# Two large constants moved to the front of the constant pool, and one narrow constant widened to 96 bytes

## The chip, the cores and the metric

The kernel runs on one core of a Trainium2 chip. The time is device microseconds (us) of one execution. Before the change the median of three runs is 2517.71 us (2516.28 to 2519.01). Engines are called as the profile calls them: PE is the matmul engine (PEld is its weight load), DVE the vector engine, ACT the scalar engine, POOL GpSimd, SP the engine that issues the DMAs.

## The reference

A decoder trunk of two layers on one sequence of 1024 tokens, model width 1024, all in float32. Every layer is: RMS norm, token mixer, residual add, RMS norm, gated MLP with a causal convolution of width 3, residual add. A final RMS norm follows.

```python
for layer in range(2):
    hn = rms_norm(h, norm_mix[layer])
    if layer == 0:
        h = h + diff_attention(hn, ...)   # 8 heads, two score maps per head, rotary positions
    else:
        h = h + gla(hn, ...)              # gated linear attention, 4 heads
    h = h + conv_ffn(rms_norm(h, norm_ffn[layer]), ...)   # 1024 -> 2 x 2816 -> 1024
return rms_norm(h, norm_final)
```

Most of the arithmetic is in the dense products: the projections of the mixers and the two matrices of each MLP.

## The kernel before

**Three matmuls for one.** Every float32 product is made of two parts with fewer bits, high and low. `mm3` (L141 to L144) adds three matmuls into one place of PSUM:

```python
nc.tensor.matmul(ps, lhsT=ah, rhs=bh, start=first, stop=False)   # L142
nc.tensor.matmul(ps, lhsT=ah, rhs=bl, start=False, stop=False)   # L143
nc.tensor.matmul(ps, lhsT=al, rhs=bh, start=False, stop=last)    # L144
```

The first operand (`lhsT`) is stationary: 128 columns of it are loaded into the array ahead of each matmul, which the profile shows as an LDWEIGHTS on PEld. The second (`rhs`) is the moving operand and streams through, mostly 512 numbers in each of 128 partitions, that is 2048 bytes of each partition. In the profile a matmul is named output<-moving,stationary: `psq<-XH,wh` streams XH against the weight `wh`.

**Where things lie in SBUF.** Each partition is laid out by tile pools one behind the other, in the order in which they are opened (L52 to L55): `const`, `wpool`, `small`, `slots`. Within a pool the tiles follow each other in the order in which the program asks for them first, and each takes a multiple of 32 bytes. As built, the first constant begins at byte 16,512 of every partition, and then

| what | bytes of a partition | begins at | over a multiple of 64 by | over a multiple of 512 by |
|---|---|---|---|---|
| `ident`, `ones_f`, `ones` | 512 each | 16,512 | 0 | 128 |
| `mhalf` (a column of -0.5) | 4, takes 32 | 18,048 | 0 | 128 |
| `XH` | 32,768 | 18,080 | 32 | 160 |
| `XL` | 32,768 | 50,848 | 32 | 160 |
| `sub`, `ls`, `lam`, `cv`, `gn`, `ba` | 864 in all | 83,616 | 32 | 160 |
| `wpool`: `st` x3, `wh` x2, `wl` x2 | 4,096 each | 84,480 | 0 | 0 |
| `small` (columns of statistics) | 1,088 | 113,152 | 0 | 0 |
| `slots`: 28 common places | 4,096 each | 114,240 | 0 | 64 |

All rows within XH, XL, `wpool` and the places begin at a whole multiple of 512 bytes from the start of their tile, so that the last column holds for every operand that is cut from them.

**XH and XL** are the normalized activations, transposed (feature in the partition, token in the row), as high and low part: 8 blocks of 1024 tokens. `norm_to_X` (L197) and `Blocks` (L234, L244) fill them. They are then the moving operand of

- the projections of both mixers, `project_T` (L146): q and k of the attention and of the GLA (`psq`), the attention's values (`psv`, 512 wide) and the GLA's gate (`psr`), each against weights in `wpool`. In `project_tok` (L153, the GLA's values, `psv` 256 wide) they are stationary instead;
- the up-projection of the MLP, `ffn` (L521). It is computed by Strassen's scheme in the variant of Winograd: seven products per pair of feature tiles instead of eight. `product` (L526) takes one of seven blocks of the activations and one of seven blocks of the weights. Four activation blocks (A11, A12, A22, S1) are cut from XH and XL, three (S2, S3, S4; `S` in the profile) lie in common places. Of every 11 weight blocks 7 lie in common places (`uw`) and 4 in `wpool` (`wh`, `wl`), by turns (L489).

**In the down-projection** XH and XL are free and serve as two more sets of places: `places` (L614) gives, for every sixth pair of feature tiles and the next, XH and XL both as stationary (the hidden activations) and as moving operand (the weights). The other four sets are common places (`gh`, `gl`, `wdh`, `wdl`). Two or three sets take turns within one accumulation (`pacc`, L318).

```python
n = f % 6
if n < 4:
    return [slot(i, z, F32R) for i, z in zip(DOWN[layer][n], ("gh", "gl", "wdh", "wdl"))]
return [z[:, 2 * (n - 4) + i, :] for i in range(2) for z in (XH, XL)]
```

**The order of the work.** The program is written out flat. The scheduler (L1344) orders instructions by its model of their times; in the up-projections and the output projections the order on PE is pinned by `in_order` (L135). All DMAs are issued on SP. Raw weights are loaded into `st` and split by ACT (the high part) and POOL (the low part).

`mhalf` is the exponent of the inverse square root in the norms: a POOL power of 128x1 numbers (L174, L191).

Of the kernel before, what the change touches and what calls it, by code (L numbers as in the profile page):

```python
# [10 lines left out]
F32 = mybir.dt.float32  # L11
F32R = mybir.dt.float32r
# [6 lines left out]
P = 128  # L19
D = 1024  # L20
T = 1024
NT = T // P
KT = D // P
# [23 lines left out]
def trunk(ctx, tc, x, norm_mix, norm_ffn, norm_final, wqk, wv, w_o, lam_in, subln,  # L47
# [4 lines left out]
    const = ctx.enter_context(tc.tile_pool(name="const", bufs=1))  # L52
# [4 lines left out]
    psm = ctx.enter_context(tc.tile_pool(name="psm", bufs=4, space=PSUM))  # L57
    dram = ctx.enter_context(tc.tile_pool(name="dram", bufs=1, space=DRAM))

    ident = const.tile([P, P], F32, name="ident")  # L60
    ones_f = const.tile([P, P], F32, name="ones_f")
    nc.vector.memset(ones_f, 1.0)
    ones = const.tile([P, P], F32R, name="ones")
    nc.vector.tensor_copy(ones, ones_f)
    mhalf = const.tile([P, 1], F32, name="mhalf")
    nc.vector.memset(mhalf, -0.5)
    XH = const.tile([P, KT, T], F32R, name="XH")
    XL = const.tile([P, KT, T], F32R, name="XL")

    o_scr = dram.tile([2 * HEADS, P, T], F32, name="o_scr")  # L70
    h_scr = dram.tile([NT, P, D], F32, name="h_scr")
# [3 lines left out]
    def f32(ap):  # L75
        return ap.bitcast(F32)

    def slot(i, name, dt=F32, shape=None):

        return slots.tile(shape or [P, 1024], dt, name=name, tag=f"s{i}")  # L80
# [60 lines left out]
    def mm3(ps, ah, al, bh, bl, first, last, **kw):  # L141
        nc.tensor.matmul(ps, lhsT=ah, rhs=bh, start=first, stop=False, **kw)  # L142
        nc.tensor.matmul(ps, lhsT=ah, rhs=bl, start=False, stop=False, **kw)  # L143
        nc.tensor.matmul(ps, lhsT=al, rhs=bh, start=False, stop=last, **kw)  # L144

    def project_T(ps, w, hf):  # L146

        wh, wl = (z.rearrange("p (k c) -> p k c", k=KT) for z in w)
        for k in range(KT):
            mm3(ps, wh[:, k, :], wl[:, k, :], XH[:, k, half(hf)], XL[:, k, half(hf)],  # L150
                k == 0, k == KT - 1)

    def project_tok(ps, w2, t):  # L153

        for k in range(KT):
            wh, wl = (z.rearrange("p (k c) -> p k c", k=4) for z in w2[k // 4])
            tok = slice(t * P, (t + 1) * P)
            mm3(ps, XH[:, k, tok], XL[:, k, tok], wh[:, k % 4, :], wl[:, k % 4, :],
                k == 0, k == KT - 1)

    def half(hf):
        return slice(512 * hf, 512 * hf + 512)
# [34 lines left out]
    def norm_to_X(hn, t):  # L197
        for g in range(2):
# [5 lines left out]
            dst = (slice(None), slice(4 * g, 4 * g + 4), slice(t * P, (t + 1) * P))  # L204
            nc.scalar.copy(XH[dst], pv)
            nc.vector.tensor_tensor(XL[dst], pv, f32(XH[dst]), op=ALU.subtract)

# [4 lines left out]
    class Blocks:  # L212
# [5 lines left out]
        def parts(self, n):  # L218
# [3 lines left out]
            d, tok = {"A11": (0, 0), "A12": (4, 0), "A22": (4, 1), "S1": (0, 1)}[n]  # L222
            return [[(0, X[:, d:d + 4, half(tok)])] for X in (XH, XL)]

# [15 lines left out]
        def first_row(self, h0, t):  # L240
# [4 lines left out]
            pv = pt.rearrange("p (a b) -> p a b", a=KT)  # L245
            hi, lo = (z[:, :, t * P:(t + 1) * P] for z in (XH, XL))
            nc.scalar.copy(hi, pv)
# [273 lines left out]
    def ffn(layer, X, last_blocks, up, gain_src, after):  # L521
# [92 lines left out]
        def places(f):  # L614
# [6 lines that stand above are left out]
# [727 lines left out]
```

## Time and profile before

| | |
|---|---|
| median of three runs | 2517.71 us (2516.28 to 2519.01) |
| profiled execution, device time | 2519.34 us |
| its span, first to last instruction | 2517.6 us |
| mean granted PE clock | 0.991 |
| PE busy, matmuls | 2450.1 us (97%), 11752 |
| PEld busy | 1995.8 us (79%) |
| DVE, POOL, ACT busy | 1625.7, 1189.4, 1040.6 us |
| DMA queue of SP | 226.64 MB, 27.3% of 16 engines |

The stages on the time axis: norm and first projections (to about 50 us), attention (to 490), its output projection (to 620), the first MLP's up-projection (to 1050) and down-projection (to 1340), the GLA with its output projection (to 1870), the second MLP's up-projection (to 2270), its down-projection and the final norm.

A matmul's row has a start and a length. Matmuls overlap: the next one starts before the row of the last one ends, so that the pace of PE is the distance from start to start, and a stretch of PE that shows as busy can still run at a better or a worse pace.

### The profile page before, as it was taken

The numbers are of one execution on the slowest core, as the hardware profiler recorded it, in microseconds if no ns is written. First come the engines' busy times: TensorE is split into PE (matmuls) and PEld (weight loads), VectorE is DVE, ScalarE is ACT, GpSimd is POOL, SyncE is SP. The second block draws the span as 40 slices with busy tenths as digits, with TensorE's granted clock in tenths as the row PEclk, the third lists the DMA queues.
The fourth block names the chain that finished last, engine by engine and source line by source line (L and its number), as shares of the span: only waits on it lengthen the run. The fifth ranks groups of instructions, "written<-read, shape, count | busy, mean of one in ns | idle before, by whom it ended". The sixth has DMA issues, their size and how long they took to land. (4 is left out here: it accounts for less than half of the span.)

```text
span 2517.6 us, 30784 instructions
## 1 busy us (share of the span) xinstructions
PE 2450.1 (97%) x11752; PEld 1995.8 (79%) x11752; DVE 1625.7 (65%) x2210; ACT 1040.6 (41%) x1630; POOL 1189.4 (47%) x723
## 2 busy tenths in 40 slices
PE   7999999998999999999999999999899999999998
PEld 6777777776788888878888998987678888887887
DVE  5577777877666666654565486487676666655455
ACT  4454544544454554432124443442345445443211
POOL 4444444425655555554423344343465555545441
PEclk9999999999999999999999999999999999999999
DMA  5222222433222222343321111124322222244331
GB/s 188 56 67 59 59 59 59 126 122 126 75 76 84 76 85 83 137 157 109 101 87 60 34 43 59 35 92 156 112 76 76 84 77 88 79 147 148 107 101 67
DMA packets 66020, 228.60 MB, mean 91 GB/s; under 512 B 8145, under 2 KB 8785, under 8 KB 65873
## 3 DMA queue, kind: packets, MB, share of 16 engines
q1 hardware_dynamic: 65872, 226.64, 27.3%
q8 instruction: 92, 1.51, 0.3%
q14 instruction: 56, 0.45, 0.1%
HBM read 163.17 MB, written 50.86 MB: 85 GB/s over the span
## 5 line engine op out<-in xcount | busy, mean ns | idle before, releaser
L325 DVE TENSOR_TENSOR res<-pacc,res 128x512 f32<-128x512 f32 x368 | 252.9, 690 | 238.1 <-PE pacc L144 237.6
L497 POOL TENSOR_TENSOR uw<-st,uw 128x512 fp32r<-128x512 f32 x190 | 290.9, 1532 | 219.8 <-ACT uw L496 212.1
L123 POOL TENSOR_TENSOR wl<-st,wh 128x1024 fp32r<-128x1024 f32 x57 | 146.0, 2568 | 203.6 <-ACT wh L122 203.6
L144 PE MATMUL pacc<-wdh,gl 128*128 128x512 f32 x512 | 200.8, 392 | 0.0
L143 PE MATMUL pacc<-wdl,gh 128*128 128x512 f32 x512 | 200.5, 392 | 0.0
L142 PE MATMUL pacc<-wdh,gh 128*128 128x512 f32 x512 | 198.6, 392 | 1.8 <-DVE res L316 1.8
L576 DVE SCALAR_TENSOR_TENSOR b<-cu,cv,b 128x1023 f32<-128x1023 f32 x44 | 63.4, 1440 | 172.5 <-ACT b L575 172.2
L496 ACT CAST uw<-st 128x512 fp32r<-128x512 f32 x190 | 118.0, 622 | 123.8 <-PE ps_z L144 54.2
L142 PE MATMUL psq<-XH,wh 128*128 128x512 f32 x384 | 156.6, 408 | 0.1
L143 PE MATMUL psq<-XL,wh 128*128 128x512 f32 x384 | 154.1, 401 | 0.1
L144 PE MATMUL psq<-XH,wl 128*128 128x512 f32 x384 | 152.6, 399 | 0.0
L626 POOL TENSOR_TENSOR gl<-st,gh 128x1024 fp32r<-128x1024 f32 x32 | 77.8, 2430 | 151.3 <-ACT gh L625 108.4
L779 ACT ACTIVATE p<-p,nmax 128x256 f32<-128x256 f32 (+7 forms) x128 | 99.1, 777 | 85.4 <-DVE nmax L776 84.2
L497 POOL TENSOR_TENSOR wh<-st,wh 128x512 fp32r<-128x512 f32 x56 | 87.1, 1555 | 80.8 <-ACT wh L496 80.8
L625 ACT CAST gh<-st 128x1024 fp32r<-128x1024 f32 x32 | 33.6, 1050 | 202.7 <-PE pacc L143 144.1
L497 POOL TENSOR_TENSOR wl<-st,wl 128x512 fp32r<-128x512 f32 x56 | 85.3, 1524 | 63.0 <-ACT wl L496 63.0
L142 PEld LDWEIGHTS pacc<-wdh,gh 128*128 128x128 f32 x512 | 96.1, 188 | 23.4 <-DVE res L316 2.6
L143 PEld LDWEIGHTS pacc<-wdl,gh 128*128 128x128 f32 x512 | 96.1, 188 | 21.7
L144 PEld LDWEIGHTS pacc<-wdh,gl 128*128 128x128 f32 x512 | 96.1, 188 | 20.9
L776 DVE CUSTOM_DVE_ANT_0 p<-s_ps,mask 128x256 f32<-128x256 f32 (+7 forms) x128 | 91.4, 750 | 30.7 <-PE pta L802 22.4
L142 PE MATMUL pacc<-wh,gh 128*128 128x512 f32 x256 | 103.2, 409 | 4.0 <-DVE res L325 4.0
L143 PE MATMUL pacc<-wl,gh 128*128 128x512 f32 x256 | 102.8, 403 | 1.5 <-POOL wl L123 1.5
(363 smaller groups left out, 7358.9 us busy)
## 6 DMA issues: line engine op xcount, KB each, us to landing
st<-in_wup_dram SPq DMA_DIRECT2D x88, 512.0 KB, 3.5
g_scr<-a SPq DMA_DIRECT2D x44, 512.0 KB, 2.6
st<-in_wdn_dram SPq DMA_DIRECT2D x44, 512.0 KB, 3.6
st<-g_scr SPq DMA_DIRECT2D x44, 512.0 KB, 3.3
r_scr<-res SPq DMA_DIRECT2D x24, 512.0 KB, 4.7
res<-r_scr SPq DMA_DIRECT2D x24, 512.0 KB, 5.7
st<-in_wqk_dram SPq DMA_DIRECT2D x16, 512.0 KB, 3.5
st<-o_scr SPq DMA_DIRECT2D x13, 512.0 KB, 3.3
```

The lines of the kernel that those rows point to most:

```text
L123: (eng_lo or nc.gpsimd).tensor_tensor(lo, st, f32(hi), op=ALU.subtract)
L142: nc.tensor.matmul(ps, lhsT=ah, rhs=bh, start=first, stop=False, **kw)
L143: nc.tensor.matmul(ps, lhsT=ah, rhs=bl, start=False, stop=False, **kw)
L144: nc.tensor.matmul(ps, lhsT=al, rhs=bh, start=False, stop=last, **kw)
L325: nc.vector.tensor_tensor(res[t][:, half(dh)], ps, res[t][:, half(dh)], op=ALU.add)
L496: nc.scalar.copy(w[:, half(0)], src)
L497: nc.gpsimd.tensor_tensor(w[:, half(1)], src, f32(w[:, half(0)]), op=ALU.subtract)
L576: nc.vector.scalar_tensor_tensor(u[:, 1:], c[:, :T - 1], cv[:, n, 1:2], u[:, 1:], op0=ALU.mult, op1=ALU.add)
L625: nc.scalar.copy(hi, st)
L626: nc.gpsimd.tensor_tensor(lo, st, f32(hi), op=ALU.subtract)
L776: nc.vector.tensor_tensor_reduce(out=pm[:, :w], in0=s_ps[:, :w], in1=st["mask"][:, T - w:], scale=-0.125, scalar=3.0e38, op0=ALU.add, op1= ...
L779: nc.scalar.activation(pm[:, :w], pm[:, :w], AF.Exp, bias=nmax, scale=-1.0, accum_out=sums[:, m:m + 1])
```

## The change

XH and XL are asked for ahead of the narrow constants, and `mhalf` becomes the first column of a tile of 24 numbers, 96 bytes, in place of 4. No instruction is added, removed or given another shape; what changes is where tiles lie.

```diff
+    XH = const.tile([P, KT, T], F32R, name="XH")
+    XL = const.tile([P, KT, T], F32R, name="XL")
     ident = const.tile([P, P], F32, name="ident")
     ones_f = const.tile([P, P], F32, name="ones_f")
     nc.vector.memset(ones_f, 1.0)
     ones = const.tile([P, P], F32R, name="ones")
     nc.vector.tensor_copy(ones, ones_f)
-    mhalf = const.tile([P, 1], F32, name="mhalf")
+    mhalf = const.tile([P, 24], F32, name="mhalf")[:, :1]
     nc.vector.memset(mhalf, -0.5)
-    XH = const.tile([P, KT, T], F32R, name="XH")
-    XL = const.tile([P, KT, T], F32R, name="XL")
```

## The prediction

> **What bounds the kernel now.** I read the page's busy times first, then the busy time by stage, then who PE waits for.
>
> ```profile
> PE 2450.1 (97%) x11752; PEld 1995.8 (79%) x11752; DVE 1625.7 (65%) x2210; ACT 1040.6 (41%) x1630; POOL 1189.4 (47%) x723
> PEclk9999999999999999999999999999999999999999
> ```
>
> PE is busy for 97% of the span and no other engine for more than 65%; the granted clock is at 90% or more in every slice. In the stages (columns: stretch, its length, then busy time and instructions of PE, PEld, DVE, ACT, POOL):
>
> ```profile
> 50.00:490.00 440.00, 429.81 (x2156) 332.74 (x2155) 320.96 (x640) 215.56 (x442) 214.83 (x147) 0.99 0.27 74
> 620.00:1050.00 430.00, 422.81 (x1818) 341.64 (x1817) 283.81 (x275) 212.79 (x317) 240.70 (x157) 0.98 0.24 81
> 1050.00:1340.00 290.00, 288.94 (x1286) 235.70 (x1285) 160.14 (x220) 73.16 (x90) 115.43 (x54) 1.00 0.36 121
> 1340.00:1830.00 490.00, 475.11 (x2839) 413.28 (x2838) 318.61 (x425) 195.07 (x277) 214.48 (x115) 0.99 0.22 73
> 1870.00:2270.00 400.00, 399.90 (x1725) 323.94 (x1724) 259.60 (x244) 196.20 (x279) 214.62 (x137) 1.00 0.27 94
> ```
>
> In the up-projections (620 to 1050, 1870 to 2270) and the down-projection PE has nearly no gap: these stages last as long as their matmuls. In attention (50 to 490) and the GLA (1340 to 1830) it idles for 2 to 3%, and rows stretched by waits add to that. What PE waits for is little, the longest sum first:
>
> ```profile
> PE pt L202 <- DVE hn L179: 12.5, 4, 8.3
> ...
> PE s_ps L766 <- DMA ks<-kl: 2.4, 1, 2.4
> ```
>
> For a DMA it waits once, for 2.4 us. So a change that adds no instruction can move the time by one thing above all: the pace at which matmuls follow each other.
>
> **The pace is not the same everywhere.** All matmuls quoted from here on stream 512 numbers against 128 columns. From the timeline (start us, length us, the rest), the first and the last row of three runs without a gap:
>
> ```profile
> 1158.13 0.39 PE L142 MATMUL pacc<-wdh,gh 128*128 128x512 f32 x1
> ...
> 1164.93 0.39 PE L142 MATMUL pacc<-wdh,gh 128*128 128x512 f32 x1
> ```
> ```profile
> 661.12 0.40 PE L142 MATMUL ps_z<-XH,uw 128*128 128x512 f32 x1
> ...
> 663.93 0.39 PE L142 MATMUL ps_x<-S,wh 128*128 128x512 f32 x1
> ```
> ```profile
> 695.58 0.40 PE L142 MATMUL ps_x<-XH,wl 128*128 128x512 f32 x1
> ...
> 698.39 0.40 PE L142 MATMUL ps_x<-S,wl 128*128 128x512 f32 x1
> ```
>
> With both operands in common places 30 matmuls take 6.80 us, 226.7 ns each. With XH and XL moving, 12 take 2.81 us, 234.2 ns each, against weights in places (`uw`) as in `wpool` (`wl`). The groups by line and shape show that this holds throughout (after the bar: busy us, mean length of one in ns; three lines are one triple):
>
> ```profile
> L142 PE MATMUL ps_z<-S,uw 128*128 128x512 f32 x112 | 43.7, 390 | 0.0
> L144 PE MATMUL ps_z<-S,uw 128*128 128x512 f32 x112 | 43.6, 390 | 0.0
> L143 PE MATMUL ps_z<-S,uw 128*128 128x512 f32 x112 | 43.6, 389 | 0.0
> ...
> L144 PE MATMUL ps_z<-XH,uw 128*128 128x512 f32 x112 | 44.4, 396 | 0.0
> L143 PE MATMUL ps_z<-XL,uw 128*128 128x512 f32 x112 | 44.2, 395 | 0.0
> L142 PE MATMUL ps_z<-XH,uw 128*128 128x512 f32 x112 | 44.2, 394 | 0.0
> ...
> L142 PE MATMUL ps_z<-XH,wh 128*128 128x512 f32 x32 | 12.7, 397 | 0.0
> L144 PE MATMUL ps_z<-XH,wh 128*128 128x512 f32 x32 | 12.7, 396 | 0.0
> L143 PE MATMUL ps_z<-XL,wh 128*128 128x512 f32 x32 | 12.7, 396 | 0.0
> ...
> L142 PE MATMUL ps_z<-S,wl 128*128 128x512 f32 x32 | 12.7, 396 | 0.0
> L144 PE MATMUL ps_z<-S,wl 128*128 128x512 f32 x32 | 12.7, 395 | 0.0
> L142 PE MATMUL ps_z<-S,wh 128*128 128x512 f32 x32 | 12.6, 393 | 0.0
> L143 PE MATMUL ps_z<-S,wl 128*128 128x512 f32 x32 | 12.6, 393 | 0.0
> L143 PE MATMUL ps_z<-S,wh 128*128 128x512 f32 x32 | 12.5, 391 | 0.0
> L144 PE MATMUL ps_z<-S,wh 128*128 128x512 f32 x32 | 12.5, 390 | 0.0
> ```
>
> A row's length is its pace plus about 162 ns (389.7 beside 226.7, 395.0 beside about 234), so a difference of lengths is, to 2 ns, a difference of pace. Same line, output and shape: places against places 389.7; XH and XL against places 395.0; places against `wpool` 393.0; XH and XL against `wpool` 396.3. What differs is where the operands lie.
>
> **Which property of the place?** Beginnings over a multiple of 512 bytes: places 64, `wpool` 0, XH and XL 160. In the down-projection and the output projections:
>
> ```profile
> L142 PE MATMUL pacc<-wdh,gh 128*128 128x512 f32 x512 | 198.6, 392 | 1.8 <-DVE res L316 1.8
> ...
> L144 PE MATMUL pacc<-XH,XL 128*128 128x512 f32 x192 | 76.0, 397 | 0.0
> L142 PE MATMUL pacc<-XH 128*128 128x512 f32 x192 | 75.6, 394 | 0.0
> L143 PE MATMUL pacc<-XL,XH 128*128 128x512 f32 x192 | 75.1, 391 | 0.0
> ```
> ```profile
> L142 PE MATMUL pacc<-wh,gh x256: 387/394/792, 492.5 to 1818.5; 128*128 128x512 f32 x128
> ...
> L143 PE MATMUL pacc<-XL,XH x192: 387/393/397, 1096.3 to 2476.6; 128*128 128x512 f32 x192
> ```
>
> (The second fence has minimum, median and maximum.) With both operands in XH and XL a matmul comes down to 387 ns, as short as any, and yet the places that take turns with them rise to 392. `wpool` moving against places has the median 394 though it begins on a multiple of 64. So "begins on a multiple of 64" isn't what decides alone. What fits every row is that a moving and a stationary row cost little where both begin at the same place within 512 bytes, more the further they differ: difference 0 (places) 389.7, +64 (places against `wpool`) 393.0, +96 and +160 (XH against either) 395.0 and 396.3.
>
> **The change part by part.** XH moves from 18,080 to 16,512 and XL from 50,848 to 49,280; `mhalf` takes 96 bytes instead of 32, so all behind it moves up by 64: `wpool` to 84,544, the places to 114,304. Over a multiple of 512 that makes XH and XL 128, places 128, `wpool` 64. The common places were on multiples of 64 already; only XH and XL weren't. Places and `wpool` keep their distance, so their rows keep their cost. XH and XL stand to the places as the places do to each other (0) and to `wpool` as the places do (+64). Where each ends:
>
> - Up-projections, XH and XL against places: 2 layers x 22 pairs x 4 products x 12 matmuls = 2112, of which 7/11 = 1344; 395.0 to 389.7 gives 5.3 ns each, 7.1 us. All on the path.
> - The same against `wpool`, 768: 396.3 to 393.0, 3.3 ns, 2.5 us, on the path.
> - Projections of attention and GLA: `psq` 1152, `psv` 384, `psr` 384, 1920 in all, at 3.3 ns 6.3 us. The median of `psq` below agrees with 396.3. Here PE shares the end with DVE and ACT chains: I take two thirds, 4.2, between 0 and 6.3.
> - Down-projection: 576 in XH and XL at a mean of 394.0 to 389.7, 2.5 us; of 1536 beside them at 392, 2.3 ns over 389.7, 3.5 us, I take half, since some excess will have other causes: 1.8.
>
> ```profile
> L142 PE MATMUL psq<-XH,wh x384: 391/397/796, 20.1 to 1632.8; 128*128 128x512 f32 x192
> ```
>
> The other engines read and write XH and XL too, and the columns of -0.5 are read by POOL:
>
> ```profile
> L626 POOL TENSOR_TENSOR gl<-st,gh x32: 2391/2416/2657, 1046.6 to 2455.9; 128x1024 fp32r<-128x1024 f32 x32
> L626 POOL TENSOR_TENSOR XL<-st,XH x24: 2392/2408/3291, 1085.8 to 2414.1; 128x1024 fp32r<-128x1024 f32 x24
> ```
> ```profile
> L174 POOL TENSOR_TENSOR rs<-ms,mhalf x39: 544/549/1614, 5.9 to 2508.8; 128x1 f32<-128x1 f32 x39
> ```
>
> The same subtraction takes 2416 ns into a place and 2408 into XL: nothing to gain there. The power keeps its 128x1 form; I put it and the DMAs' new destinations at nothing, since PE waits for a DMA for 2.4 us in all; were all forty powers dearer by a tenth and on the path, it would be 40 x 0.055 = 2.2 us.
>
> Sum: 7.1 + 2.5 + 4.2 + 4.3 = 18.1 us. The profiled execution took 2519.34 us, so 2501.2; the median of the runs lies 1.6 below it, so 2499.6, rounded **2500 us**. Bounds: only a third of the sum, 2512; all of every term, and XH against `wpool` down to 389.7 (2688 x 6.6 = 17.7), with 7.1 and 6.0: 30.8 us, 2487.
>
> **Rivals.**
>
> *The moving row alone decides, by where it begins within 128 bytes.* Now the places begin 64 over, `wpool` 0, XH and XL 32 over; 64 would be the good one. For it: `wpool` moving has 394 where places have 389.7. Then the change turns the good value over from the places to `wpool`: 1008 matmuls of the up-projections go from 389.7 to 395.0 (5.3 us), 576 from 393.0 to 396.3 (1.9), 1536 of the down-projection from 392 to 395.0 (4.6), and some 528 with `wpool` moving gain 5 ns (2.6). Together 9.2 us: **2527 us, slower**. Against it: the 387 of XL, a moving row 32 over, and the places' 392 beside XH. It decides if the first triple above, places against places, comes out at 395.
>
> *The beginning doesn't matter; what does is the tile or its region,* which stays nearly where it was. Then 2518, no change. Against it: the places, which begin 1 KB behind `wpool`'s end, have another pace than it. The Trainium skill, SBUF — State Buffer, section Specifications (TRN2), gives lines of 16 bytes, of which every beginning here, before and after, is a multiple. TensorE: Matmul & The Clock Gate, Part 2, says that PE has two separate read ports, so that loading the next weights takes nothing from the running matmul. By either the sum would be 0 and the time stay; the 5.3 ns between rows of one shape disagree with the two taken as the whole story.
>
> *A smaller gain,* 5 to 8 us: the pace improves by the multiple of 64 alone, or phases within a triple eat the rest; 2511.
>
> **How the numbers follow.** The forecast has 0.60, the smaller gain 0.10, no change 0.15, the slower one 0.15. A measurement tells about 0.2% (5 us) from no change: faster 0.70, same 0.15, slower 0.15. The forecast's own range is 2487 to 2512; taking in the smaller gain and no change, 2490 to 2521 leaves out the slower rival and the far low end.
>
> **What would show it.** Right: XH and XL moving in `ps_z` at about 390 against `uw` and 393 against `wh`, `psq` at a median of 393 to 394, the `pacc` triples of XH at 390, places against places still 389.7, the second up-projection some 5 us shorter than 400. Wrong: `ps_z<-S,uw` at 395, or `ps_z<-XH,uw` unmoved, or a better pace of PE that comes back as waits for DVE or ACT in attention.

## The result and the profile after

The changed kernel takes 2487.57 us (median; 2486.8 to 2489.78), the kernel before, on the same chip, 2517.01 us. The ratio is 0.9889, 95% interval 0.9877 to 0.9901: 29.4 us less, where 18 were forecast: just below the low end of the range on record (2490), and at the end of the forecast's own range (2487). All matmuls stand in the same order on PE, so the two traces can be laid over each other instruction by instruction; lines of the kernel after stand one higher (L143 to L145 for the triple). Its profiled execution took 2486.8 us. Two executions are in none of the figures below, one of the changed kernel that took 2670 us at a granted clock of 0.848 and one of the kernel before that took 7827 us.

The page of the kernel after, its busy times and the granted clock:

```profile
PE 2410.0 (97%) x11752; PEld 1986.8 (80%) x11752; DVE 1631.9 (66%) x2210; ACT 1037.3 (42%) x1630; POOL 1195.9 (48%) x723
PEclk9999999999999999999999999999999999999999
```

The share of PE is the same 97%: the span shrank because PE does the same 11752 matmuls in less time, 40.1 us less, and not because it waits less. It waits more: the span less PE's busy time was 67.5 us before and is 75.0 us now, so that the span is only 32.6 us shorter. Where the gain came from, the busy times by stage show. The edges are set at the same instructions at which the stages were cut before, so that each row holds the same work (the length of the stretch is the first number behind the edges):

```profile
49.52:483.96 434.44, 422.51 (x2156) 330.61 (x2155) 319.66 (x640) 215.45 (x442) 217.53 (x147) 1.00 0.27 75
615.02:1036.09 421.07, 412.86 (x1818) 339.14 (x1817) 287.51 (x275) 211.16 (x317) 243.83 (x157) 0.99 0.24 83
1036.09:1321.89 285.80, 284.64 (x1286) 235.66 (x1285) 159.85 (x220) 73.16 (x90) 115.11 (x54) 1.00 0.37 123
1321.89:1806.89 485.00, 467.62 (x2839) 408.56 (x2838) 318.59 (x424) 194.57 (x275) 211.68 (x114) 0.99 0.22 72
1848.44:2241.12 392.68, 392.68 (x1724) 323.99 (x1724) 262.87 (x243) 194.55 (x279) 216.15 (x137) 1.00 0.28 95
...
483.96:615.02 131.06, 121.95 (x586) 96.40 (x584) 94.28 (x152) 54.14 (x95) 43.97 (x33) 0.97 0.36 119
1806.89:1848.44 41.55, 35.22 (x154) 28.47 (x153) 29.14 (x29) 18.47 (x34) 27.03 (x18) 0.93 0.21 75
2241.12:2485.00 243.88, 236.00 (x1040) 194.74 (x1038) 129.76 (x178) 53.80 (x62) 100.68 (x48) 0.99 0.31 104
```

The last of these stretches, in the kernel before:

```profile
2270.00:2517.60 247.60, 239.70 (x1040) 194.72 (x1038) 129.79 (x178) 53.79 (x62) 100.57 (x48) 1.00 0.31 102
```

Against the stretches before (440, 430, 290, 490, 400, 130, 40 and 247.6 us) attention gains 5.6 us, the up-projections 8.9 and 7.3, the down-projections 4.2 and 3.7 and the GLA 5.0; 0.5 comes from the first 50 us. The two stretches with the output projections give back 1.1 and 1.6 (the first at a granted clock of 0.97, before 0.99). Together that is 32.5 us, the difference of the two profiled executions (2519.34 and 2486.8).

Not all of it is the change. The traces record stretches in which the granted clock was half of the full one: up to the last matmul 44.4 us of them before and 30.7 us after. The matmuls that start in or beside them took 5.3 us less in the kernel after, 3.0 of it in attention and 2.5 in the first up-projection. The pad alone (below), with all distances as before, has 37.5 us of such stretches, so they vary without any change of distance. The medians, 29.4 us apart, rest on several runs.

The three runs of the forecast, at the same instructions, in the timeline of the kernel after (start us, length us):

```profile
1142.64 0.39 PE L143 MATMUL pacc<-wdh,gh 128*128 128x512 f32 x1
...
1149.44 0.39 PE L143 MATMUL pacc<-wdh,gh 128*128 128x512 f32 x1
...
653.88 0.39 PE L143 MATMUL ps_z<-XH,uw 128*128 128x512 f32 x1
...
656.60 0.39 PE L143 MATMUL ps_x<-S,wh 128*128 128x512 f32 x1
...
688.51 0.39 PE L143 MATMUL ps_x<-XH,wl 128*128 128x512 f32 x1
...
691.25 0.39 PE L143 MATMUL ps_x<-S,wl 128*128 128x512 f32 x1
```

Places against places: 30 in 6.80 us, 226.7 ns, as before. XH and XL against places: 12 in 2.72 us, 226.7 ns (234.2 before). XH and XL against `wpool`: 12 in 2.74 us, 228.3 ns (234.2 before). In the groups by line and shape:

```profile
L144 PE MATMUL pacc<-wdl,gh 128*128 128x512 f32 x512 | 198.9, 389 | 0.0
...
L143 PE MATMUL pacc<-XH 128*128 128x512 f32 x192 | 74.7, 389 | 0.0
...
L145 PE MATMUL pacc<-XH,XL 128*128 128x512 f32 x192 | 74.4, 389 | 0.0
...
L143 PE MATMUL ps_z<-S,uw 128*128 128x512 f32 x112 | 43.7, 390 | 0.0
...
L143 PE MATMUL ps_z<-XH,uw 128*128 128x512 f32 x112 | 43.6, 389 | 0.0
...
L143 PE MATMUL ps_z<-XH,wh 128*128 128x512 f32 x32 | 12.5, 392 | 0.0
...
L143 PE MATMUL ps_z<-S,wh 128*128 128x512 f32 x32 | 12.5, 392 | 0.0
```

XH and XL now have the lengths of the places beside which they stand: 389 against `uw`, 392 against `wh`, 389 in the down-projection, where also the places between them came down, from 392 to 389 or 390. Places against places stay at 389 to 390, which alone ends the rival of a moving row that decides by itself. The longest of PE's waits, and its one wait for a DMA, are about what they were (us in total, times, longest; 12.5 and 2.4 before). Waits for ACT and DVE between them grew (the two lines in the middle were 3.7 and 1.1 before):

```profile
PE pt L203 <- DVE hn L180: 12.7, 4, 8.8
...
PE ps_x L143 <- ACT rv L557: 5.2, 2, 2.7
PE ssp L295 <- DVE hl L286: 4.5, 9, 1.1
...
PE s_ps L767 <- DMA ks<-kl: 2.6, 1, 2.6
```

By stage, the stretch less PE's busy time went from 10.2 to 11.9 us in attention, from 14.9 to 17.4 in the GLA and from 4.2 to 6.3 in the short stretch ahead of the second up-projection.

### The profile page after: what moved, and what is told of

It reads as the page before. It is cut to its first block, busy times and chain, and to the rows that moved or that the text cites. A ratio compares the mean times of both kernels' runs of the same rounds, so it can differ in the third digit from the quotient of the medians.

```text
span 2485.0 us, 30784 instructions
## 1 busy us (share of the span) xinstructions
PE 2410.0 (97%) x11752; PEld 1986.8 (80%) x11752; DVE 1631.9 (66%) x2210; ACT 1037.3 (42%) x1630; POOL 1195.9 (48%) x723
## 5 line engine op out<-in xcount | busy, mean ns | idle before, releaser
L143 PE MATMUL pacc<-wdh,gh 128*128 128x512 f32 x512 | 197.9, 390 | 1.9 <-DVE res L317 1.9
L145 PE MATMUL pacc<-wdh,gl 128*128 128x512 f32 x512 | 199.3, 389 | 0.0
L497 ACT CAST uw<-st 128x512 fp32r<-128x512 f32 x190 | 117.9, 621 | 114.4 <-PE ps_z L145 50.9
L143 PE MATMUL psq<-XH,wh 128*128 128x512 f32 x384 | 154.7, 403 | 0.1
L145 PE MATMUL psq<-XH,wl 128*128 128x512 f32 x384 | 150.7, 394 | 0.0
L143 PEld LDWEIGHTS pacc<-wdh,gh 128*128 128x128 f32 x512 | 96.1, 188 | 22.5 <-DVE res L317 2.7
L145 PEld LDWEIGHTS pacc<-wdh,gl 128*128 128x128 f32 x512 | 96.1, 188 | 20.1
L143 PE MATMUL pacc<-wh,gh 128*128 128x512 f32 x256 | 103.6, 411 | 4.0 <-DVE res L326 4.0
```

What stands on the lines that cost most here:

```text
L497: nc.scalar.copy(w[:, half(0)], src)
```

## The experiments

The theories, in short. **A**, the forecast's: what counts is the distance from the beginning of the stationary row to that of the moving row, over a multiple of 512. **B**: rows are cheap where they begin on a multiple of 64 bytes. **C**: the moving row alone decides, by its place within 128 bytes.

### The law, measured by itself

This kernel leaves the trunk out. 48 matmuls of each kind run on two tiles that begin a whole multiple of 512 bytes apart; the moving rows begin `dm` numbers, the stationary rows `ds` numbers behind a multiple of 512 bytes from the start of their tile. `P` is 128, `n` 512 and `count` 48; the cut shows the loop alone.

```diff
+            for j in range(count):
+                a, b = ds + P * (j % 8), dm + 512 * (j % 8)
+                nc.tensor.matmul(ps[:, :n], lhsT=st[:, a:a + P], rhs=mv[:, b:b + n], start=j == 0, stop=j == count - 1)
```

> Leaves the whole trunk out (it copies rows of x to the output) and streams nothing but matmuls of one shape, 128 columns stationary against 512 moving numbers: 48 in a row for each pair of beginnings, the moving row shifted by 0 to 480 bytes in steps of 32 with the stationary row fixed (m.sa), the stationary row shifted with the moving one fixed (mas.), both shifted together (m.s. with equal letters), the moving row shifted by 4, 8, 16 and 24 bytes (mv_one, two, four, six), and the first series again with 256 moving numbers (half). Theory A (the difference of the two beginnings counts, zero is best): all pairs with equal letters run at 226 to 227 ns like masa, also those that begin 32 over a multiple of 64; shifts of one of the two cost 2 to 10 ns, about 2 at +64 and 6 at -64. Theory B (what counts is that the moving row begins on a multiple of 64 bytes): every second letter of the moving row is slow by 5 ns or more whatever the stationary row does, mbsb and mdsd too, and moves by 64 or 128 bytes cost nothing. Theory C (the moving row alone counts, 64 over a multiple of 128 is best): masc to maso are all alike, and the moving series alternates with a period of 128 bytes.

Its timeline has one row for each kind (start, us from the first start to the last end). The letter behind `m` is the place of the moving row, that behind `s` of the stationary one: a is 0, b 32 bytes, c 64, e 128, g 192, i 256; `mv_one` is 4 bytes:

```profile
24.05 11.04 PE L49 MATMUL masa<-mv,st 128*128 128x512 f32 x48
34.93 11.37 PE L49 MATMUL mbsa<-mv,st 128*128 128x512 f32 x48
46.13 11.16 PE L49 MATMUL mcsa<-mv,st 128*128 128x512 f32 x48
...
68.34 11.36 PE L49 MATMUL mesa<-mv,st 128*128 128x512 f32 x48
...
113.16 11.05 PE L49 MATMUL misa<-mv,st 128*128 128x512 f32 x48
...
213.47 11.36 PE L49 MATMUL masc<-mv,st 128*128 128x512 f32 x48
...
258.27 11.16 PE L49 MATMUL masg<-mv,st 128*128 128x512 f32 x48
...
369.53 11.08 PE L49 MATMUL mbsb<-mv,st 128*128 128x512 f32 x48
...
533.24 11.42 PE L49 MATMUL mv_one<-mv,st 128*128 128x512 f32 x48
```

Less the last row's length (0.39 us) and divided by 47, the pace is 226.6 ns at distance 0, 233.6 at 32 bytes, 229.1 at 64, 233.4 at 128, 226.8 at 256. With the stationary row at 64 (distance -64) it is 233.4, at 192 (-192, which is +64 over a multiple of 256) 229.1. Both rows 32 bytes off a multiple of 64: 227.4. Four bytes of distance already cost the full price, 234.7. So B and C fall here: in a stream of one kind only the distance counts, and it counts over a multiple of **256**, not 512. "More the further they differ" falls too: there are three prices, about 227 at 0, 229 at +64, and 232 to 235 at everything else tried. Each kind ran once, in one execution.

### Half of the change: the order alone, the pad alone

The order of the changed kernel, with `mhalf` narrow again (XH and XL 128, places 64, `wpool` 0 over a multiple of 512):

```diff
-    mhalf = const.tile([P, 24], F32, name="mhalf")[:, :1]
+    mhalf = const.tile([P, 1], F32, name="mhalf")
```

> XH and XL first, mhalf left at 4 bytes: XH and XL begin 128 over a multiple of 512, the places 64, the weight pool 0, all on multiples of 64; XH stands 64 above the places and 128 above the weight pool. Theory A: XH against places goes from 226.9 back to about 229 to 230 ns a matmul and to 233 where XH is stationary, XH against the weight pool (128 apart) is unknown between 229 and 234; the time 2495 to 2512. Theory B: all begins are on multiples of 64, so the time is that of the changed kernel, 2488 within 4. Theory C: places stay at the good 64, only XH is as slow as before: about 2517.

Measured: 2509.34 us (2506.33 to 2511.25), ratio 0.9967 (0.9954 to 0.9979). Every row lies on a multiple of 64 as in the changed kernel, and about three quarters of the gain are missing; B wanted 2488. XH and XL now stand 64 from the places and 128 from `wpool`.

The pad alone, in the order of before (XH and XL 224, places 128, `wpool` 64: all distances as before):

```diff
-    mhalf = const.tile([P, 1], F32, name="mhalf")
+    mhalf = const.tile([P, 24], F32, name="mhalf")[:, :1]
```

> mhalf widened, the order of before: XH and XL begin at 224 over a multiple of 512, the places at 128, the weight pool at 64; every difference is that of the kernel before, and XH is still 32 over a multiple of 64. Theory A and theory B: 2517 within 4, no change from before. Theory C: the places lose the good 64, slower, about 2527.

Measured: 2518.1 us (2515.26 to 2518.92), ratio 1.0 (0.9991 to 1.0009). Everything behind `mhalf` moved by 64 bytes and nothing changed. C, which wanted 2527, falls in the trunk as well. The pad does nothing by itself; with the new order it brings XH and XL to distance 0 from the places.

### All in one phase

The pad at 40 numbers, and one tile of statistics with two buffers instead of four, which shortens `small` by 64 bytes: XH, XL, places and `wpool` all at 128.

```diff
-    mhalf = const.tile([P, 24], F32, name="mhalf")[:, :1]
+    mhalf = const.tile([P, 40], F32, name="mhalf")[:, :1]
...
-        ss = small.tile([P, 2], F32, name="ss2")
+        ss = small.tile([P, 2], F32, name="ss2", bufs=2)
```

> Order of the change, mhalf at 160 bytes and the column pair ss2 with two buffers instead of four, so that XH, XL, the weight pool and the places all begin 128 over a multiple of 512. Theory A: matmuls with one operand in the weight pool fall to 227 as well: 2688 from 229.4 (6.5 us), 576 from 228.9 (1.1), 528 from 233.4 (3.4), 11 us in all, 2477. Theory B and theory C: 2488 within 4, as the changed kernel.

Measured: 2484.5 us (2481.56 to 2488.3), ratio 0.9866 (0.985 to 0.9882). A's forecast of 2477 was too low, B's 2488 too high by as little as the measurement tells, so this run separates nothing. The next does: the same, but with everything 32 bytes past a multiple of 64 (`mhalf` ahead of XH, 40 numbers behind `ones_f`).

```diff
+    mhalf = const.tile([P, 1], F32, name="mhalf")
     XH = const.tile([P, KT, T], F32R, name="XH")
     XL = const.tile([P, KT, T], F32R, name="XL")
...
-    ones_f = const.tile([P, P], F32, name="ones_f")
+    ones_f = const.tile([P, P + 40], F32, name="ones_f")[:, :P]
...
-    mhalf = const.tile([P, 24], F32, name="mhalf")[:, :1]
...
-        ss = small.tile([P, 2], F32, name="ss2")
+        ss = small.tile([P, 2], F32, name="ss2", bufs=2)
```

> XH/XL, common places and wpool slots all begin 32 bytes past a multiple of 64, and all at the same phase (160 past a multiple of 512): no row lies on a multiple of 64, but every distance is 0. Theory A (distance modulo 256 decides): as the one-phase kernel on multiples of 64, 2482 to 2488 us. Theory B (multiples of 64 decide, as the change says of itself): no gain, 2515 to 2520 us.

Measured: 2484.6 us (2484.09 to 2485.42), ratio 0.9873 (0.9858 to 0.9888). Not one of these rows begins on a multiple of 64, and the kernel is as fast as the one on multiples of 64. B is refuted; a beginning on a multiple of 64 is not the cause of the gain. Groups by line and shape of this kernel:

```profile
L143 PE MATMUL ps_z<-XH,uw 128*128 128x512 f32 x112 | 43.6, 389 | 0.0
...
L143 PE MATMUL ps_z<-XH,wh 128*128 128x512 f32 x32 | 12.4, 389 | 0.0
```

Even `wh`, at 392 in the changed kernel, comes down to 389, since its distance is 0 now. The changed kernel itself, beside it on the same chip:

> The changed kernel once more, beside the variants of this job, to compare them on one chip: 2487 us by every theory.

Measured: 2487.38 to 2489.65 us, ratio 0.9887 (0.9872 to 0.9902). All four runs of the one-phase kernel 32 bytes off lie below these, by some 4 us, though the intervals of the two ratios overlap. A's count for one phase was 11 us. In the trace of the kernel 32 bytes off PE's idle time is 78.5 us, against 75.0 in the changed kernel; whether the faster matmuls or the two buffers for `ss2` caused that, no run separates.

### XH and XL moved away again, by 128 and by 256 bytes

Places and `wpool` at distance 0 of each other, XH and XL 128 away from both, all on multiples of 64 (`mhalf` 72 numbers wide), and then 256 away (104 wide). Against the changed kernel:

```diff
-    mhalf = const.tile([P, 24], F32, name="mhalf")[:, :1]
+    mhalf = const.tile([P, 72], F32, name="mhalf")[:, :1]
...
-        ss = small.tile([P, 2], F32, name="ss2")
+        ss = small.tile([P, 2], F32, name="ss2", bufs=2)
```

> XH/XL at 128, places and wpool slots at 256 past a multiple of 512: all on multiples of 64, places and slots at distance 0 of each other, XH/XL at distance 128 from both. Theory A: the pairs of XH/XL with slots and places cost 233.4 ns instead of 226.7 to 228.9, 1376 with places by 6.5 and 2688 with slots by 4.2 ns = 20 us more than the changed kernel, the place-slot pairs (576 + 1536 by 2 to 4.5 ns = 8 us at most) are cheaper: 2497 to 2510 us. Theory B: all on multiples of 64, as the changed kernel, 2487 us or a little less.

Measured: 2504.85 us (2503.85 to 2506.38), ratio 0.9953 (0.994 to 0.9965), within A's 2497 to 2510 and far from B's 2487. By group:

```profile
L143 PE MATMUL ps_z<-XH,uw 128*128 128x512 f32 x112 | 44.2, 395 | 0.0
...
L143 PE MATMUL ps_z<-XH,wh 128*128 128x512 f32 x32 | 12.6, 395 | 0.0
...
L143 PE MATMUL ps_z<-S,wh 128*128 128x512 f32 x32 | 12.4, 389 | 0.0
```

> XH/XL at 128, places and slots at 384 past a multiple of 512: XH/XL 256 bytes away from both. If the distance counts modulo 512, as the prediction took it, XH/XL pairs pay the full 233.4 ns and the kernel takes 2500 to 2510 us, as with a distance of 128. If it counts modulo 256, as the single pairs showed, this is the one-phase kernel: 2482 to 2488 us.

Measured: 2484.53 us (2478.79 to 2485.8), ratio 0.9867 (0.9847 to 0.9887). A period of 512 bytes wanted 2500 to 2510. So in the trunk, too, the distance counts over a multiple of 256. Between these two kernels only the distance of XH and XL to all the rest differs, by 128 bytes: 20 us.

### Whose stationary row, and how wide

PEld is busy for 80% of the changed kernel's span and PE for 97%, so stationary rows are loaded while matmuls run. Does the distance to a matmul's own stationary row count, or that to the next one's? Here two kinds of stationary rows alternate, 128 bytes apart (64 in `own_quarter`, which is built like `own`); the trunk is left out. `dm` and `ds` are pairs now, in numbers of 4 bytes; the cut shows three of the kinds and the line that picks the rows.

```diff
+    yield "own", (0, 32), (0, 32), 512, COUNT
+    yield "next", (32, 0), (0, 32), 512, COUNT
...
+    yield "half", (0, 0), (0, 32), 512, COUNT
...
+                a, b = ds[j % 2] + P * (j % 8), dm[j % 2] + 512 * (j % 8)
```

> The trunk is left out again: 48 matmuls of each kind on two tiles of random rows, outputs not the trunk's. Two kinds of stationary rows alternate, at 0 and at 128 bytes. Theory A with the distance to the matmul's OWN stationary rows: 'own' (moving rows follow their own: 0, 128) runs at 226.7 ns, 'next' (moving 128, 0: distance 128 to its own, 0 to the rows loaded for the next matmul) at 233.4 ns, 'half' (moving always 0) at the mean, 230. Rival, the distance to the stationary rows that are LOADED DURING the matmul, which are the next one's: 'next' 226.7, 'own' 233.4, 'half' 230. The quarter kinds (distance 64 bytes between the two stationaries): own 226.7 against next 228.9 to 233.4, or the other way round. By size (128, 256, 384, 512 columns), distance 0, 64 and 128: a cost by column would give 3.3 ns at 256 columns where 512 have 6.7; a cost by load of 128 columns would give the same ns at each size, unless the load hides. After 48 matmuls at a distance of 160 bytes, 48 at distance 0 in eight groups of 6: if the rows get well at once, all groups run at 226.7 ns; if a lag lingers, as the unchanged place-by-place rows of the trunk suggest (228.2 before, 227.0 after), the first groups are dearer.

From its timeline (`size_..._b` are 256 wide, at distance 0 and +64):

```profile
29.75 5.97 PE L54 MATMUL size_zero_b<-mv,st 128*128 128x256 f32 x48
60.13 5.87 PE L54 MATMUL size_plus_b<-mv,st 128*128 128x256 f32 x48
...
126.74 11.14 PE L54 MATMUL own<-mv,st 128*128 128x512 f32 x48
137.71 11.20 PE L54 MATMUL next<-mv,st 128*128 128x512 f32 x48
...
159.79 11.31 PE L54 MATMUL half<-mv,st 128*128 128x512 f32 x48
170.94 11.28 PE L54 MATMUL own_quarter<-mv,st 128*128 128x512 f32 x48
...
226.63 1.56 PE L54 MATMUL other_a<-mv,st 128*128 128x512 f32 x6
```

In the way worked out above: own 228.7 ns, next 230.0, half 232.3. Neither theory has this: 226.7 against 233.4, one way or the other, was expected. With stationary rows 64 bytes apart, own costs 231.7 and next 233.4. So the distance to the own stationary row isn't the whole of it where phases change from one matmul to the next, and why stays open.

The price of +64 isn't fixed either. `other_a` to `other_h` are eight groups of six at +64, right behind 48 matmuls at 160 bytes: from start to start they run at 233.0 to 233.4 ns, not at 229. What ran before and the groups of six both differ from the stream of 48, and no run separates them.

The trunk has the same in the down-projections. There the moving and the stationary row of a matmul always come from the same set, so that their distance is 0 before and after the change; only the sets that take turns were 96 bytes apart before. Yet, taken from start to start over all matmuls that don't wait, those in XH and XL went from 232.4 to 226.7 ns and those in places from 229.4 to 226.8.

With 256 columns the order even turns round: distance 0 is the dearer (a pace of about 121 ns, +64 about 119; 119.6 and 117.9 in the kernel with the pairs).

### What a dear pair leaves behind

Triples as in `mm3`: twelve at a distance, then groups `a` to `d` of three triples at distance 0, three times over; the trunk is left out.

```diff
+for name, dm in DIST.items():            # 0, 64, 96, 128, 160, 192 bytes
+    for again in range(3):
+        run("x_" + name, dm, 12)
+        for part in "abcd":
+            run("s_%s_%s" % (name, part), 0, 3)
```

> The trunk is left out again. In the changed kernel the up-projection's rows between two places (distance 0 before and after) got cheaper too, 395 to 400 ns to 390 to 392 ns. Here triples as the trunk issues them (the same stationary rows twice, then others): twelve triples at a distance d, then four groups of three triples at distance 0, for d of 0, 64, 96, 128, 160 and 192 bytes, three times each; then single triples at d and at 0 by turns. Theory A alone (own distance decides, nothing stays): every group at distance 0 has 389 to 390 ns of row length whatever came before. Rival, a lag that stays after a dear pair until TensorE next waits: the groups at distance 0 after d of 64 to 192 show 392 to 400 ns, those after d = 0 show 389.

Groups by line and shape, first matmul of the triples, after triples at 64 bytes (`quarter`), at 96 (`threeeighths`) and at 0 (`none`):

```profile
L34 PE MATMUL s_quarter_a<-mv,st 128*128 128x512 f32 x9 | 3.6, 397 | 0.0
...
L34 PE MATMUL s_threeeighths_a<-mv,st 128*128 128x512 f32 x9 | 3.6, 395 | 0.0
L34 PE MATMUL s_quarter_b<-mv,st 128*128 128x512 f32 x9 | 3.5, 390 | 0.0
...
L34 PE MATMUL s_none_a<-mv,st 128*128 128x512 f32 x9 | 3.5, 389 | 0.0
...
L34 PE MATMUL s_threeeighths_b<-mv,st 128*128 128x512 f32 x9 | 3.5, 389 | 0.0
```

Something lingers: the first three triples at distance 0 still show 395 to 397, the next three are back at 389 to 390. The tail depends on the distance before it. From start to start the nine matmuls of group `a` cost, over 226.7 ns, 5.1 ns each after 64 bytes and 4.2 after 96, but only 1.7 to 2.2 after 128, 160 and 192. In the kernel with the alternating rows, six at distance 0 right behind 48 single matmuls at 160 bytes cost 0.5 ns each over 226.7, nearly nothing. Where single triples at 64 bytes and at 0 take turns, those at 0 stay dear throughout (rows of 390 to 399 ns). In the trunk the same appears in the places against places that stand beside XH and XL. The first matmul of their triples in `ps_x`, from the groups of the kernel before (XH and XL 96 away):

```profile
L142 PE MATMUL ps_x<-S,uw 128*128 128x512 f32 x224 | 89.5, 400 | 0.1
```

with the order alone (64 away):

```profile
L143 PE MATMUL ps_x<-S,uw 128*128 128x512 f32 x224 | 89.6, 400 | 0.2 <-ACT r L560 0.2
```

in the changed kernel (0 away):

```profile
L143 PE MATMUL ps_x<-S,uw 128*128 128x512 f32 x224 | 87.9, 392 | 0.0
```

and in the kernel with XH and XL 128 away:

```profile
L143 PE MATMUL ps_x<-S,uw 128*128 128x512 f32 x224 | 87.7, 391 | 0.0
```

With XH and XL 96 and 64 bytes away these rows have 400, with 0 and 128 they have 392 and 391, though their own distance is 0 in all four. That fits the tail; that it is the same effect is argued, not shown.

## Why the prediction was right and wrong

**Right: what bounds, the direction, and the kind of law.** The stages that last as long as their matmuls shrank, and no DMA took the gain back. That beginnings matter as a distance between the two operands, and not each by itself, holds in every run, with the limit that the distance to the own stationary row isn't the whole of it where phases take turns. The signs named for "right" came out but for their size: `ps_z` at 389 and 392, `psq` at a median of 394, `pacc` at 389, places against places unmoved, the second up-projection 7.3 us shorter instead of "some 5". One sign named for "wrong" came out in part: PE's idle time grew by 1.7 us in attention and by 7.5 in all.

**Wrong: the period, which did no harm.** All rows of the kernel before fit 256 as well as 512. "More the further they differ" was read from 393.0, 395.0 and 396.3; in streams of one kind it is about a third of the price for +64 and one full price for the rest.

**Wrong: the size, 18.1 us for 29.4 in the medians.** The measured column takes the two traces matmul by matmul: from the start of each to the start of the next, before less after. Distances above 260 ns in either trace count as waits, and matmuls in or beside a stretch at half clock stand by themselves. From the first matmul to the last the sum is 33 us.

| term | forecast, us | measured, us |
|---|---|---|
| up-projections, XH and XL against places | 1344 x 5.3 ns = 7.1 | 9.0 (233.8 to 226.8 ns) |
| up-projections, XH and XL against `wpool` | 768 x 3.3 ns = 2.5 | 3.8 (233.8 to 228.9 ns) |
| up-projections, places beside them | not counted | 2.9 (1.6 to 2.0 ns each) |
| attention and GLA, 512 wide | 6.3, two thirds of it: 4.2 | 7.3 (3.6 to 4.1 ns each) |
| GLA values, 256 wide | not counted | 3.3 (below) |
| down-projections, XH and XL | 2.5 | 3.3 (232.4 to 226.7 ns) |
| down-projections, places beside them | 3.5, half of it: 1.8 | 4.0 (229.4 to 226.8 ns) |
| all other matmuls | 0 | 0.7 |
| longer waits of PE | in the third above | -6.5 |
| stretches at half clock | 0 | 5.3 |

- *The step that failed first* is "a difference of lengths is, to 2 ns, a difference of pace". The 2 ns are of the size of the prices themselves, and entered neither the sum nor the bounds. The forecast had the pace, 234.2 against 226.7, and used the lengths of `ps_z`, 395.0 against 389.7: 5.3 ns where the pace fell by 7.0, and 3.3 where it fell by 4.9 against `wpool`. Over these two and the whole terms of attention, the GLA and the down-projections, the prices so taken came out 5.5 us too low.
- *The discounts.* Half for the places beside XH in the down-projection was caution with no row behind it, and "some excess will have other causes" was wrong: they came down to 389 or 390 entirely. That is 1.7 us. The third taken off in attention and the GLA, 2.1 us, was a guess, too, but not too much: distances above 260 ns grew by 4.1 us there, and by 6.5 us in all. What was too small is what it was taken from.
- *What wasn't counted.* The places beside XH and XL in the up-projections, and the GLA's values, 6.2 us together. The values, 256 wide with XH and XL as stationary, went from a distance of 96 to one of 192 (-64). One of the three rows, from the groups of the kernel before:

```profile
L143 PE MATMUL psv<-wl,XH 128*128 128x256 f32 x256 | 72.3, 282 | 2.0 <-POOL wl L123 2.0
```

and of the kernel after:

```profile
L144 PE MATMUL psv<-wl,XH 128*128 128x256 f32 x256 | 71.3, 279 | 1.1 <-POOL wl L124 1.1
```

From start to start their pace fell from 124.2 to 119.9 ns, over 768 matmuls 3.3 us. The one-phase kernels, where these rows stand at distance 0, have rows of 283 there and a pace of 123.7: with 256 columns 0 is no good place, as the pairs by themselves showed. These 2.9 us, and 3.5 us more of PE's idle time, are most of the gap between the 4 us that one phase brought and the 11 that A expected.

**The rivals.** The moving row alone: refuted by the pad alone (2518.1, not 2527) and by the pairs. No change: refuted by the result; distances of 32, 64 and 128 bytes, all multiples of 16, cost 233.6, 229.1 and 233.4 ns where 0 costs 226.6. The sentence of the Trainium skill, TensorE: Matmul & The Clock Gate, Part 2, that loading the next tile's weights doesn't steal read bandwidth from the running matmul, isn't the whole story here: the pace goes from 226.6 to 233.4 ns where only the beginning of the stationary row changes (`masc`). Whether the load costs this, no run shows. The smaller gain by the multiple of 64: refuted by the one-phase kernel 32 bytes off (2484.6). The upper bound of the sum, 2487, is the time that came, but by luck: it has 17.7 us for XH and XL against `wpool`, where 11.1 came (3.8 and 7.3), and leaves out the places beside, the values and the waits. The range on record had been cut to 2490 on that side, to take in cases that the rows spoke against on the other.

**Open.** Why the distance matters at all, why +64 is cheaper than -64 and in one series wasn't, and what the tail and the alternating pairs have in common. The runs give the price, not the mechanism.

## What to carry to other kernels

Where PE is busy throughout, look at the pace of matmuls of one shape from start to start, group by operand: if it differs, compare where the moving and the stationary rows begin, over a multiple of 256 bytes, and bring all operands that take turns in a stream to one phase by the order of the tiles or a pad. For rows of 512 float32 numbers that was worth about 3% of a matmul and 1.1 to 1.3% of this kernel; a multiple of 64 as such was worth nothing, and for rows of 256 numbers the best distance was another. Price such a change by the pace itself, count every row of every shape that the move touches and the rows that stand beside them, and take off what other engines will hold up: here some 34 us of pace met 6.5 us of longer waits.

## What was not expected of the hardware

- In a stream of one kind, 512 columns wide, the distance between the two operands' beginnings sets the pace over a multiple of 256 bytes: 226.7 ns at 0, 229 at +64, 232 to 235 at all else tried, 4 bytes included. Behind a series at 160 bytes, groups of six at +64 ran at 233.
- Where two phases take turns, matmuls at distance 0 to their own stationary row cost 228.7 ns (128 bytes apart) and 231.7 (64 bytes apart).
- A stream of dear pairs leaves a tail on cheap ones of up to nine matmuls, 1.7 to 5.1 ns each; in the second group of three triples at most 0.4 ns were left.
- With 256 columns distance 0 was not the best: 121 ns, against 119 at +64. With 128 columns it made no difference: 110.6 ns at 0, 64 and 128 bytes.
